# A decoder layer on one core: memory exponentials behind the value copies, rotation on VectorE, weight sums beside local attention, value transposes earlier

## The chip, the cores and the metric

One core of a Trainium2 chip runs the whole layer as one program. The metric is device microseconds of one execution; lower is better. The engines are TensorE (PE in the profile; PEld its weight loads), VectorE (DVE), ScalarE (ACT), GpSimd (POOL) and SyncE (SP), which only issues transfers. Each works through its own queue in order; what an instruction needs of another engine it waits for at the head of its queue.

## The reference, cut to what matters

The layer has a first feed-forward half step, a mixer of three branches (a recurrence, RWKV-7; sliding-window attention with rotary positions; cross-attention into 256 memory tokens), and a second feed-forward half step, for 1024 tokens of width 1024 in float32.

```
q_s = partial_rope(q_s, cos, sin); k_s = partial_rope(k_s, cos, sin)   # 16 of 64 dims of each head rotate
y_a = rwkv7_mix(p_rwkv, ...)                                           # state update token by token
y_b = sliding_window_gqa_sinks(q_s, k_s, v_s, sinks)                   # blocks of 128, the block and the one before
s = einsum('bshd,bmhd->bhsm', q * 128 ** -0.5, km); y_c = softmax(s) @ vm   # memory cross-attention
merged = g_a * (y_a @ w_branch[0]) + g_b * (y_b @ w_branch[1]) + g_c * (y_c @ w_branch[2])
h = h + rms_norm(merged @ w_out)
f2 = swiglu(rms_norm(h), ffn2_w_in, ffn2_w_out)
```

## The kernel before

**Products.** Large matrix products use a block form with 7 products where the plain one has 8, so sums of weight blocks and of activations are made first. Each factor is split into a high and a low part (`w_hi` by ACT at L304, `w_lo` by DVE at L306), and `mm3` (L381 to L383) gives three matmuls for each step of a product. The weight blocks arrive in five tiles `w_raw` by SP's queue; some eight operands (`OPS = 8`) are made ahead of PE. The accumulators lie in PSUM's eight banks, four for the large products (px, py, pz, po, pgate, pb, msc, mptr, mpv ...) and four for the rest (y, z, gram, bkt, sc, ptr, vtr, pv); a bank is taken again once its last reader is done.

**Order.** A scheduler lays down each engine's queue when the program is built. `high_priority(offset=...)` brings an instruction forward, `issue_after(x)` puts it behind x, `keep_in_program_order` fixes PE's order.

**The places of the change,** in the order of time:

- `win_pair` makes two strips of the mixer's input projection out of 7 products of 12 matmuls each (px, py, pz by turns). ACT copies px and pz into `part` (L1483), DVE adds `part` to the next accumulator into `att` (L1490), and ACT gives gates their tanh (L1493). Of its twelve pairs the seventh to the eleventh run beside `beside_pairs`, a generator from which the pairs draw one step (`between()`) behind each product. Its steps: three units of sums of the second feed-forward's output weights (for each, four loads of 256 KB, four adds on DVE at L675 to L678, four stores); the rotation's angle tables (`rope_tables`, two Sin activations on ACT, L1686 the second); and ten rotations of half a row, 128 x 512 each. A rotation (`rotate`, L1692 to L1694) is two multiplies and an add; those of row 0 (two) are made by DVE, the other eight by GpSimd. GpSimd's queue stores each (L720), and SP's loads the next half-row with its swapped copy into one of two pairs of buffers (`rope_x`, `rope_sw`).
- `rwkv_chain` goes through 16 chunks of 64 tokens. In a chunk PE makes z and y, the next chunk's value products (`values`, into the bank of y, which ACT copies to sv and uv at L1277), grams, and transposes (`turned`, bkt at L1297, which ACT copies to bk). Beside the chunks run eight `MemoryBlock`s of the cross-attention, one every two chunks: scores msc in chunk 2i + 1, maxima and four Exp activations (`powers`, L207) in the next (through the table `copied`, called once z is copied), the shares on DVE, then transposes and values.
- `attention` takes the eight blocks of the sliding window. Behind each block's scores (sc, L102) and transposes (ptr, L105) it puts some matmuls of the gate and branch products (`fill`, 46 steps a block, `LUMP = 46`). `turn_values` makes the transposes of v (vtr, L1961, two banks), two copies on ACT (vt, L1962) and a difference on DVE; it stands behind block 0's transposes.

Of the kernel before, what the change touches and what calls it, by code (L numbers as in the profile page):

```python
# [11 lines left out]
F32 = mybir.dt.float32  # L12
F32R = mybir.dt.float32r
I32 = mybir.dt.int32
ALU = mybir.AluOpType
# [3 lines left out]
P = 128  # L19
# [23 lines left out]
PAIR_UNITS = 3  # L43
# [137 lines left out]
class MemoryBlock(Block):  # L181
# [18 lines left out]

    def powers(self):
        V, S, st = self.nc.vector, self.nc.scalar, self.st
        scale = float(128 ** -0.5)
        V.tensor_scalar(st[:, 1], st[:, 0], -scale, None, ALU.mult)
        self.pr = self.pool.tile([P, 4, MEM], F32, tag="mp", name="mp", bufs=2)
        for i in range(4):
            S.activation(self.pr[:, i], self.banks[i // 2][:, (i % 2) * MEM : (i % 2 + 1) * MEM], ACT.Exp, scale=scale,  # L207
                         bias=st[:, 1, i : i + 1], accum_out=st[:, 2, i : i + 1])
# [27 lines left out]
class Builder:  # L236
# [364 lines left out]
    def ffn_in(self, f, x, form_d, first_d, parts, norm):  # L601

        nc, V = self.nc, self.nc.vector
        with self.tc.tile_pool(reuse_waits="tile", name="ffn_in", bufs=2) as pool:
# [13 lines left out]
            for j in range(KF):  # L618
                *pair, made = self.ffn_in_pair(f, j, pool, first_d)
                pairs.append(pair)  # L620
                skip = PAIR_UNITS if f == "ffn2" else 0
# [60 lines left out]
    def beside_pairs(self, pool, att_d):  # L682

        nc, V, G = self.nc, self.nc.vector, self.nc.gpsimd
# [3 lines left out]
        blocks = [t.rearrange("p (k c) -> p k c", c=P) for t in xs + sws]  # L688
# [22 lines left out]
        load(0)  # L711
        load(1)
        yield
        next(tables)
        yield
        for i, (row, h) in enumerate(rows):
            cols = slice(h * TH, (h + 1) * TH)
            self.rotate(V if row == 0 else G, xs[i % 2], sws[i % 2], cos[:, cols], sin[:, cols])
            yield
            nc.gpsimd.dma_start(att_d[row][:, cols], xs[i % 2])  # L720
            if i + 2 < len(rows):
                load(i + 2)
            if row:
                yield
# [522 lines left out]
    def rwkv_chain(self, pool, early, fetched, pk_d, inv_d, y, beside, copied, slot):  # L1247
# [23 lines left out]
        def values(n, ps):  # L1271

            for p, q in pairs:
                valued = mm(at(ps, p, 1 - q, W4), n["f"][ROWS[q], p, 4, :], self.center[ROWS[q]])
            for t in ("sv", "uv"):
                for q in (0, 1):
                    S.copy(n[t][ROWS[1 - q], q], v3(ps, W4)[ROWS[1 - q]])  # L1277
            return valued
# [40 lines left out]
        for c in range(NC_):  # L1319
# [25 lines left out]
            if not last:  # L1345
                values(nxt, py)
# [321 lines left out]
    def rope_tables(self, n, ang):  # L1668
# [6 lines left out]
        V.tensor_scalar(ang, ang, self.rope_c[:, 0:1], None, ALU.mult)  # L1675
        magic = 12582912.0
# [3 lines left out]
        for c in TWO_PI_PARTS:  # L1680
            V.scalar_tensor_tensor(ang, n, -c, ang, ALU.mult, ALU.add)
        V.tensor_scalar(ang, ang, 3.1415925, -3.1415925, ALU.min, ALU.max)
        V.scalar_tensor_tensor(n, ang, -1.0, ang, ALU.mult, ALU.max)
        yield
# [5 lines left out]
    def rotate(self, engine, x, sw, cos, sin):  # L1690

        engine.tensor_tensor(x, x, cos, ALU.mult)  # L1692
        engine.tensor_tensor(sw, sw, sin, ALU.mult)
        engine.tensor_tensor(x, x, sw, ALU.add)  # L1694
# [27 lines left out]
    def attention(self, blocks, turn_values):  # L1722

        self.fill(LUMP // 2, blocks[0].scores())
        blocks[0].soft(())
        for i, block in enumerate(blocks):
# [13 lines left out]
            if i == 0:  # L1740
                turn_values()
# [6 lines left out]
    def beside_chunks(self, i, block, copied, slot):  # L1748
# [7 lines left out]
        def scores():  # L1756
            block.scores()
            with self.tc.issue_after(self.kept.ins):
                for a in (0, 1) if late else (0,):
                    self.kept = block.most(a)  # L1760
                if late:
                    block.powers()
# [73 lines left out]
    def mixer(self, u, cp, close_raws, att_d, gate_d, km_d, vm_d):  # L1836
# [23 lines left out]
        with tc.tile_pool(reuse_waits="tile", name="gates", bufs=2) as gp:  # L1860
# [40 lines left out]
            with chunks, small("chain_y") as y_pool, small("memory") as mem_pool:  # L1901
                y = y_pool.tile([P, NPAIR, T], F32, name="y", bufs=1)
                blocks = [MemoryBlock(self, mem_pool, b, att_d=att_d, km=km, vm=vm, ahead=ahead, y_d=y_d[2]) for b in range(nb)]
                beside, copied, slot = {0: [lambda: nc.sync.dma_start(km, km_d), blocks[0].load, blocks[1].load, lambda: nc.sync.dma_start(vm, vm_d)]}, {}, {}
                for i, block in enumerate(blocks):
                    if i > 1:
                        beside[2 * i - 2] = [block.load]
                    self.beside_chunks(i, block, copied, slot)
# [8 lines left out]
                with small("chain") as pool:  # L1917
                    last = self.rwkv_chain(pool, early, fetched, pk_d, inv_d, y, beside, copied, slot)
# [26 lines left out]
            with stay, tc.tile_pool(reuse_waits="tile", name="att", bufs=1) as ap, tc.tile_pool(name="attw", bufs=2) as pool:  # L1945
# [7 lines left out]
                v_in = opened.enter_context(tc.tile_pool(reuse_waits="tile", name="v", bufs=1)).tile([P, T], F32, name="v_in")  # L1953
# [11 lines left out]
                self.attention(windows, turn_values)  # L1965
# [209 lines left out]
```

## Time and profile before

| | us |
|---|---|
| median of 3 runs | 2259.3 (2258.69 to 2261.74) |
| the profiled execution | 2259.9 |
| its span | 2258.2 |
| mean granted PE clock | 0.997 |
| ACT, busy | 1051.1 (47%) |
| POOL, busy | 118.7 (5%) |
| moved by DMA | 437.13 MB, 194 GB/s |

The profile covers one execution. A row of a timeline gives the start, the duration, the engine, the line of the kernel and the operation, and in brackets the idle time of that engine just before it with what ended it. Rows of ACTq or SPq are instructions of an engine's sequencer, mostly transfers that it issues. The pairs beside the rotation run from about 1040 to 1160 us, the chain from about 1185 to 1300, local attention from about 1315 to 1460.

### The profile page before, as it was taken

The page shows a single profiled execution, that of the slowest core. Times are in us where ns is not written, and L with a number is a line of the kernel's source. Part 1 is how long each engine was busy: PE and PEld are TensorE (multiplying, and loading weights), DVE is VectorE, ACT ScalarE, POOL GpSimd, SP SyncE. Part 2 cuts the span into 40 slices and gives each one's busy share as a digit, 9 for nine tenths or more (in the row PEclk, how much of TensorE's full clock was granted, in tenths as well). Part 3 has the DMA queues.
Part 4 walks back from the last instruction along what each step waited for, and adds up shares of the span by engine and source line. Part 5 has one row for each costly group of instructions (what it writes and reads, how often), then busy time and mean ns, then how long its engine had stood idle before and what let it go on. Part 6 is the DMA issues. An engine that isn't in the chain of part 4 may idle for free.

```text
span 2258.2 us, 34561 instructions
## 1 busy us (share of the span) xinstructions
PE 2217.0 (98%) x12244; PEld 1822.4 (81%) x12244; DVE 1680.1 (74%) x2790; ACT 1051.1 (47%) x1967; POOL 118.7 (5%) x187
## 2 busy tenths in 40 slices
PE   8999999999999999999999999999999999999998
PEld 6888888888887788888778877788888888888887
DVE  6988777766698887866747786794898887776676
ACT  6622333454556654444545574444663223345451
POOL 0000000000000011000432210000000000000000
PEclk9999999999999999999999999999999999999999
DMA  8565566686665456456664374464565555677763
GB/s 284 175 204 170 198 213 212 229 293 210 191 210 185 125 150 211 154 166 195 210 218 146 112 228 141 149 230 135 175 209 181 192 188 196 228 234 261 217 197 120
DMA packets 273628, 437.13 MB, mean 194 GB/s; under 512 B 51184, under 2 KB 89072, under 8 KB 273200
## 3 DMA queue, kind: packets, MB, share of 16 engines
q1 hardware_dynamic: 250752, 396.33, 54.4%
q10 hardware_dynamic: 20624, 34.94, 4.7%
q0 software_dynamic: 2080, 3.67, 0.5%
q8 instruction: 96, 1.57, 0.3%
q14 instruction: 76, 0.62, 0.1%
HBM read 295.90 MB, written 138.94 MB: 193 GB/s over the span
## 4 chain that ended last, share of the span: by engine, by line
PE 89%; DVE 5%; ACT 3%; DMA 2%; issue 1%; SPq 0%; ACTq 0%; DVEq 0%
PE px L381 9%; PE px L383 9%; PE px L382 9%; PE po L381 6%; PE po L383 6%; PE po L382 6%; PE pz L381 4%; PE pz L383 4%; PE pz L382 4%; PE pb L381 2%; PE pb L382 2%; PE pb L383 2%; PE pr L381 2%; PE pr L382 2%; PE pr L383 2%; PE pw L382 1%
## 5 line engine op out<-in xcount | busy, mean ns | idle before, releaser
L304 ACT CAST w_hi<-w_raw 128x512 fp32r<-128x512 f32 x618 | 382.3, 620 | 736.5 <-PE px L382 197.0
L306 DVE TENSOR_TENSOR w_lo<-w_raw,w_hi 128x512 fp32r<-128x512 f32 x618 | 428.6, 695 | 189.8 <-ACT w_hi L304 177.0
L381 PE MATMUL po<-u,w_hi 128*128 128x512 f32 (+1 forms) x476 | 180.9, 380 | 0.0
L382 PE MATMUL po<-u,w_hi 128*128 128x512 f32 (+1 forms) x476 | 180.9, 380 | 0.0
L383 PE MATMUL po<-u,w_lo 128*128 128x512 f32 (+1 forms) x476 | 180.9, 380 | 0.0
L381 PE MATMUL pz<-u,w_hi 128*128 128x512 f32 x400 | 156.0, 390 | 0.7 <-ACT part L1483 0.7
L381 PE MATMUL px<-u,w_hi 128*128 128x512 f32 x400 | 155.8, 390 | 0.8 <-DVE km L1658 0.8
L383 PE MATMUL px<-u,w_lo 128*128 128x512 f32 x400 | 155.8, 389 | 0.0
L383 PE MATMUL pz<-u,w_lo 128*128 128x512 f32 x400 | 155.7, 389 | 0.0
L382 PE MATMUL pz<-u,w_hi 128*128 128x512 f32 x400 | 155.6, 389 | 0.0
L382 PE MATMUL px<-u,w_hi 128*128 128x512 f32 x400 | 155.6, 389 | 0.0
L381 PE MATMUL px<-f,w_hi 128*128 128x512 f32 x352 | 137.2, 390 | 0.3 <-DVE up L783 0.3
L383 PE MATMUL px<-f,w_lo 128*128 128x512 f32 x352 | 137.0, 389 | 0.0
L382 PE MATMUL px<-f,w_hi 128*128 128x512 f32 x352 | 137.0, 389 | 0.0
L490 DVE TENSOR_TENSOR u<-hid,u 128x512 fp32r<-128x512 f32 x114 | 78.3, 689 | 47.2 <-ACT u L489 46.4
L382 PEld LDWEIGHTS po<-u,w_hi 128*128 128x128 f32 x476 | 89.5, 188 | 17.2
L383 PEld LDWEIGHTS po<-u,w_lo 128*128 128x128 f32 x476 | 89.5, 188 | 17.0
L381 PEld LDWEIGHTS po<-u,w_hi 128*128 128x128 f32 x476 | 89.5, 188 | 16.8
L489 ACT CAST u<-hid 128x512 fp32r<-128x512 f32 x114 | 70.7, 620 | 65.8 <-DMA hid<-form_d 57.7
L381 PEld LDWEIGHTS px<-u,w_hi 128*128 128x128 f32 x400 | 75.1, 188 | 17.0 <-ACT r L489 1.6
L381 PEld LDWEIGHTS pz<-u,w_hi 128*128 128x128 f32 x400 | 75.2, 188 | 16.7 <-ACT part L1483 1.1
L383 PEld LDWEIGHTS pz<-u,w_lo 128*128 128x128 f32 x400 | 75.1, 188 | 15.7
(461 smaller groups left out, 5265.0 us busy)
## 6 DMA issues: line engine op xcount, KB each, us to landing
w_raw<-in_ffn_in SPq DMA_DIRECT2D x224, 256.0 KB
hid<-form_d SPq DMA_DIRECT2D x154, 256.0 KB
w_raw<-in_win SPq DMA_DIRECT2D x112, 256.0 KB
form_d<-g SPq DMA_DIRECT2D x88, 256.0 KB
w_raw<-ffn_sum_d SPq DMA_DIRECT2D x88, 256.0 KB
ws<-in_ffn_out SPq DMA_DIRECT2D x76, 256.0 KB
ffn_sum_d<-ws SPq DMA_DIRECT2D x76, 256.0 KB
form_d<-h SPq DMA_DIRECT2D x66, 256.0 KB
```

Source lines behind the costliest of these rows:

```text
L304: self.nc.scalar.copy(hi, x)
L306: self.split_last = self.nc.vector.tensor_tensor(lo, x, hi.bitcast(F32), ALU.subtract)
L381: mm(out, wh, xh, start=first, stop=False, **kw)
L382: mm(out, wh, xl, start=False, stop=False, **kw)
L383: self.last_mm = mm(out, wl, xh, start=False, stop=last, **kw)
L489: self.nc.scalar.copy(hi, x)
L490: self.nc.vector.tensor_tensor(lo, x, hi.bitcast(F32), ALU.subtract)
```

## The change

1. In the chain, the four Exps of a memory block stand behind the next chunk's four value copies in ACT's queue instead of ahead of them; the small DVE operation ahead of them (`least`) stays where it was.
2. All ten rotations are made by VectorE. The tables come first, in six steps instead of four, with the two Sin activations next to each other; each rotation takes two steps. With the sums gone the whole takes 26 steps instead of 32.
3. The three units of weight sums leave `beside_pairs` and go to `attention`: loads in blocks 0, 2 and 4, adds and stores in blocks 1, 3 and 5, in four tiles `ws`. `PAIR_UNITS` is renamed `BLOCK_UNITS`.
4. `turn_values` stands behind block 0's scores and fill, ahead of block 1's scores.

```diff
@@ MemoryBlock
+    def least(self):
+        self.nc.vector.tensor_scalar(self.st[:, 1], self.st[:, 0], -float(128 ** -0.5), None, ALU.mult)
+
     def powers(self):
-        V, S, st = self.nc.vector, self.nc.scalar, self.st
+        S, st = self.nc.scalar, self.st
         scale = float(128 ** -0.5)
-        V.tensor_scalar(st[:, 1], st[:, 0], -scale, None, ALU.mult)
...
@@ beside_pairs
-        tables = self.rope_tables(cos, sin)
-        for q in range(PAIR_UNITS):
-            self.sums_loads("ffn2", q, blocks)
-            if q == 0:
-                next(tables)
-            yield
-            yield
-            self.sums_made("ffn2", q, blocks, self.split_last)
-            yield
-            if q < 2:
-                next(tables)
-            yield
         for t in sws:
-            G.memset(t, 0.0)
-        rows = [(0, h) for h in (0, 1)] + [(j, h) for j in range(2, 6) for h in (0, 1)]
+            nc.gpsimd.memset(t, 0.0)
+        rows = [(row, h) for row in (0, 2, 3, 4, 5) for h in (0, 1)]
...
-        load(0)
-        load(1)
-        yield
-        next(tables)
-        yield
+        for n, _ in enumerate(self.rope_tables(cos, sin)):
+            yield
+            if n in (4, 5):
+                load(n - 4)
         for i, (row, h) in enumerate(rows):
             cols = slice(h * TH, (h + 1) * TH)
-            self.rotate(V if row == 0 else G, xs[i % 2], sws[i % 2], cos[:, cols], sin[:, cols])
+            self.rotate(xs[i % 2], sws[i % 2], cos[:, cols], sin[:, cols])
             yield
             nc.gpsimd.dma_start(att_d[row][:, cols], xs[i % 2])
             if i + 2 < len(rows):
                 load(i + 2)
-            if row:
-                yield
+            yield
@@ rwkv_chain
-        def values(n, ps):
+        def values(n, ps, powers=()):
...
             for t in ("sv", "uv"):
                 for q in (0, 1):
-                    S.copy(n[t][ROWS[1 - q], q], v3(ps, W4)[ROWS[1 - q]])
+                    end = S.copy(n[t][ROWS[1 - q], q], v3(ps, W4)[ROWS[1 - q]])
+            with self.tc.issue_after(end.ins):
+                for f in powers:
+                    f()
...
-                values(nxt, py)
+                values(nxt, py, powers.get(c, ()))
@@ rope_tables
...
         V.scalar_tensor_tensor(n, ang, -1.0, ang, ALU.mult, ALU.max)
-        yield
         nc.scalar.activation(ang, ang, ACT.Sin)
         nc.scalar.activation(n, n, ACT.Sin, scale=-1.0, bias=self.half_pi)
...
-    def rotate(self, engine, x, sw, cos, sin):
-
-        engine.tensor_tensor(x, x, cos, ALU.mult)
-        engine.tensor_tensor(sw, sw, sin, ALU.mult)
-        engine.tensor_tensor(x, x, sw, ALU.add)
+    def rotate(self, x, sw, cos, sin):
+
+        V = self.nc.vector
+        V.tensor_tensor(x, x, cos, ALU.mult)
+        V.tensor_tensor(sw, sw, sin, ALU.mult)
+        V.tensor_tensor(x, x, sw, ALU.add)
@@ attention
-    def attention(self, blocks, turn_values):
+    def attention(self, blocks, turn_values, units):
 
         self.fill(LUMP // 2, blocks[0].scores())
+        turn_values()
         blocks[0].soft(())
...
                 blocks[i + 1].soft(block.copied)
-            if i == 0:
-                turn_values()
+            units[i % 2]()
             self.fill(LUMP - first, mm)
@@ beside_chunks
         if not late:
             add(copied, c + 1, lambda: block.most(1))
-            add(copied, c + 1, block.powers)
+            add(copied, c + 1, block.least)
+            add(powers, c + 1, block.powers)
@@ where attention is called
+                sums, loaded = iter(range(BLOCK_UNITS)), []
+
+                def load_unit():
+                    for q in itertools.islice(sums, 1):
+                        loaded.append((q, self.sums_loads("ffn2", q, self.sums_tiles(v_pool))))
+
+                def make_unit():
+                    while loaded:
+                        self.sums_made("ffn2", *loaded.pop(), self.split_last)
+
+                self.attention(windows, turn_values, (load_unit, make_unit))
```

In the order the rows have a line, an operation, what is written and read (numbers of buffers are given where they differ), and a shape. The changed kernel's lines are shifted: L1277 is L1264 there, L1297's copy to bk L1288, L207 L209, L1490 L1480, L1692 to L1694 L1686 to L1688, L306 L308, L331 to L337 L333 to L339, L1962 L1959, L1530 L1520, L489 L491.

ACT in the chain, from one chunk's output copy (y) on; before:

```order
L1308 COPY y<-y 128x4x64
L207 ACTIVATE mp,mst<-msc,mst 128x256 x4
L1277 COPY sv<-y 64x256 x2
L1277 COPY uv<-y 64x256 x2
L1298 COPY bk<-bkt 128x512
L1781 COPY yo<-mpv 128x512
L1782 DMA y_d<-yo 512x1x128
L1308 COPY y<-y 128x4x64
L1277 COPY sv<-y 64x256 x2
```

and now:

```order
L1298 COPY y<-y 128x4x64
L1264 COPY sv<-y 64x256 x2
L1264 COPY uv<-y 64x256 x2
L209 ACTIVATE mp,mst<-msc,mst 128x256 x4
L1288 COPY bk<-bkt 128x512
L1777 COPY yo<-mpv 128x512
L1778 DMA y_d<-yo 512x1x128
L1298 COPY y<-y 128x4x64
L1264 COPY sv<-y 64x256 x2
L1264 COPY uv<-y 64x256 x2
L1288 COPY bk<-bkt 128x512
```

The four Exps (mp) have gone from ahead of sv and uv to behind them, and ahead of bk.

DVE beside the fourth of these five pairs of products; before:

```order
L331 TENSOR_TENSOR part<-w_raw 128x512
L306 TENSOR_TENSOR w_lo<-w_raw,w_hi 128x512
L332 TENSOR_TENSOR w_raw<-w_raw 128x512
L1490 TENSOR_TENSOR att<-py,part 128x512
L333 TENSOR_TENSOR w_raw<-part,w_raw 128x512
L337 TENSOR_TENSOR w_raw<-w_raw 128x512
L306 TENSOR_TENSOR w_lo<-w_raw,w_hi 128x512
L306 TENSOR_TENSOR w_lo<-part,w_hi 128x512
L306 TENSOR_TENSOR w_lo<-w_raw,w_hi 128x512
L1490 TENSOR_TENSOR att<-px,part 128x512
```

and now:

```order
L1686 TENSOR_TENSOR rope_x_9898<-rope_x_9898,cos 128x512
L308 TENSOR_TENSOR w_lo<-w_raw,w_hi 128x512
L333 TENSOR_TENSOR part<-w_raw 128x512
L308 TENSOR_TENSOR w_lo<-w_raw,w_hi 128x512
L334 TENSOR_TENSOR w_raw<-w_raw 128x512
L1687 TENSOR_TENSOR rope_sw_9900<-rope_sw_9900,sin 128x512
L1480 TENSOR_TENSOR att<-py,part 128x512
L335 TENSOR_TENSOR w_raw<-part,w_raw 128x512
L1688 TENSOR_TENSOR rope_x_9898<-rope_x_9898,rope_sw_9900 128x512
L339 TENSOR_TENSOR w_raw<-w_raw 128x512
L308 TENSOR_TENSOR w_lo<-w_raw,w_hi 128x512
L308 TENSOR_TENSOR w_lo<-part,w_hi 128x512
```

Before, only weight operands (w_lo, part, w_raw) and the adds of att stood there, while GpSimd rotated; now the operations of the rotations stand between them, in the same queue.

ACT in local attention round the copies of vt; before:

```order
L163 COPY pt<-ptr 128x512
L489 CAST u<-yin 128x512
L148 ACTIVATE st<-st 128x8
L150 ACTIVATE sc,st<-sc,st 128x128 x5
L304 CAST w_hi<-w_raw 128x512
L150 ACTIVATE sc,st<-sc,st 128x128 x3
L1962 COPY vt<-vtr 128x512 x2
L1530 ACTIVATE gate<-pgate,half_gb 128x512
L131 COPY sc<-sc 128x256 x4
L304 CAST w_hi<-w_raw 128x512 x2
```

and now:

```order
L150 ACTIVATE sc,st<-sc,st 128x128
L148 ACTIVATE st<-st 128x8
L150 ACTIVATE sc,st<-sc,st 128x128 x7
L1520 ACTIVATE gate<-pgate,half_gb 128x512
L1810 DMA gin<-gate_d 128x512
L1959 COPY vt<-vtr 128x512 x2
L491 CAST u<-yin 128x512
L131 COPY sc<-sc 128x256
L1810 DMA gin<-gate_d 128x512
L131 COPY sc<-sc 128x256
```

The vt copies stood behind the eight Exps of block 1; now they stand behind those of block 0, ahead of the copies of block 1's scores (L131). On PE the eight vtr transposes, which stood directly behind block 0's ptr, stand directly ahead of block 1's sc.

More of the change, by code (lines that the diff above doesn't have):

```diff
@@ L42 @@
 KEEP = KP - OPS
-PAIR_UNITS = 3
+BLOCK_UNITS = 3
 RAWS = 5
@@ L682, in beside_pairs @@
     def beside_pairs(self, pool, att_d):
-        nc, V, G = self.nc, self.nc.vector, self.nc.gpsimd
+        nc = self.nc
         cos, sin = (pool.tile([P, T], F32, name=n, bufs=1) for n in ("cos", "sin"))
@@ L1903, in mixer @@
                 blocks = [MemoryBlock(self, mem_pool, b, att_d=att_d, km=km, vm=vm, ahead=ahead, y_d=y_d[2]) for b in range(nb)]
-                beside, copied, slot = {0: [lambda: nc.sync.dma_start(km, km_d), blocks[0].load, blocks[1].load, lambda: nc.sync.dma_start(vm, vm_d)]}, {}, {}
+                beside, copied, powers, slot = {0: [lambda: nc.sync.dma_start(km, km_d), blocks[0].load, blocks[1].load, lambda: nc.sync.dma_start(vm, vm_d)]}, {}, {}, {}
                 for i, block in enumerate(blocks):
@@ L1917, in mixer @@
                 with small("chain") as pool:
-                    last = self.rwkv_chain(pool, early, fetched, pk_d, inv_d, y, beside, copied, slot)
+                    last = self.rwkv_chain(pool, early, fetched, pk_d, inv_d, y, beside, copied, powers, slot)
                     self.held = []
@@ L1963, in turn_values @@
                     nc.vector.tensor_tensor(vd, vt[:, 1:], vt[:, : T // P - 1], ALU.subtract)
-                self.attention(windows, turn_values)
+                sums, loaded = iter(range(BLOCK_UNITS)), []
[6 more added lines that the diff above has]
+                self.attention(windows, turn_values, (load_unit, make_unit))
+                assert not loaded and next(sums, None) is None
                 for _ in self.fills:
```

19 lines of the change are left out of this document (12 added, 7 removed).

## The prediction

> **What bounds the kernel now.** I read the page first, for which engine is full; then PE's waits, for what the few idle microseconds wait for; then the timelines of PE and of the releasing engine round each of those waits.
>
> ```profile
> span 2258.2 us, 34561 instructions
> PE 2217.0 (98%) x12244; PEld 1822.4 (81%) x12244; DVE 1680.1 (74%) x2790; ACT 1051.1 (47%) x1967; POOL 118.7 (5%) x187
> ```
>
> TensorE (PE) is busy for all but 41.2 us of the span. The change takes no matmul away, so it can gain only idle time of PE and what a slower clock costs behind it. PE's waits, by releaser (total, times, longest):
>
> ```profile
> PE bkt L1297 <- ACT uv L1277: 7.5, 7, 1.1
> ...
> PE px L381 <- ACT part L1483: 6.1, 4, 2.5
> PE sc L102 <- ACT vt L1962: 2.2, 1, 2.2
> ...
> PE pz L381 <- ACT part L1483: 0.7, 1, 0.7
> ...
> PE z L1257 <- DVE sv L1355: 0.2, 1, 0.2
> ```
>
> What the change can reach is 7.5 in the chain, 6.1 + 0.7 beside the rotation, and 2.2 in local attention: 16.5 us. A wait can cost more than itself, which the clock shows (columns: window; busy time of PE, PEld, DVE, ACT, POOL; granted PE clock; DMA share; GB/s):
>
> ```profile
> 1120.00:1140.00 20.00, 17.30 (x68) 13.54 (x67) 15.14 (x12) 6.87 (x12) 16.93 (x15) 0.91 0.53 176
> 1330.62 0.39 PE L382 MATMUL pgate<-u,w_hi 128*128 128x512 f32 x1
> ...
> 1333.79 0.39 PE L381 MATMUL pgate<-u,w_hi 128*128 128x512 f32 x1
> ...
> 1131.05 0.39 PE L383 MATMUL pz<-mix_form,w_lo 128*128 128x512 f32 x1
> 1133.97 0.50 PE L381 MATMUL px<-mix_form,w_hi 128*128 128x512 f32 x1 [2.53 <-ACT part L1483]
> ...
> 1138.42 0.40 PE L381 MATMUL pz<-u,w_hi 128*128 128x512 f32 x1
> ```
>
> From 1330.62 to 1333.79 lie 14 matmuls in PE's steady stream, 0.2264 us each; a product of 12 takes 2.72. The 12 behind the wait of 2.53 took 1138.42 - 1133.97 = 4.45, so 1.73 more, at a granted clock of 0.91 for that window. Refilling PE costs a little too: 1131.05 to 1133.97 is 2.92, less the wait of 2.53 and a step of 0.23 leaves 0.16. The page "TensorE: Matmul & The Clock Gate" of the Trainium skill (the states table of its Part 1) has the clock drop after an idle window of about 3.4 us; by that a wait of 2.53 would leave the clock alone, and the sum below would be some 3 us smaller; here the rows decide.
>
> **Part 1: rotation by VectorE alone.** VectorE (DVE), GpSimd (POOL) and ScalarE (ACT) at the same moment:
>
> ```profile
> 1104.66 3.53 DVE L332 TENSOR_TENSOR w_raw<-w_raw 128x512 f32<-128x512 f32 x1
> 1108.11 0.68 DVE L1490 TENSOR_TENSOR att<-py,part 128x512 f32<-128x512 f32 x1
> 1109.92 3.49 DVE L337 TENSOR_TENSOR w_raw<-w_raw 128x512 f32<-128x512 f32 x1
> 1104.48 0.58 POOL L720 DMA_DIRECT2D att_d<-rope_x  x1 [0.30 <-POOL rope_x L1694]
> ...
> 1110.34 1.28 POOL L1692 TENSOR_TENSOR rope_x<-rope_x,cos 128x512 f32<-128x512 f32 x1
> 1108.82 0.72 ACT L1493 ACTIVATE att<-att,half_gb 128x512 f32<-128x512 f32 x1 [5.64 <-DVE att L1490]
> ```
>
> An addition of two SBUF tiles, 0.68 as a rule, takes 3.5 beside GpSimd's multiplies. The add of att (L1490) stands behind it in DVE's queue, the tanh behind that on ACT, and behind the tanh the copy of px that frees PE's bank; that is three of the four waits of px. The fourth is another chain on ACT: two Sin activations apart from each other, each with a table load in and out.
>
> ```profile
> 1080.40 1.28 ACT L1493 ACT_TABLE_LOAD   x1
> ...
> 1085.12 0.50 PE L381 MATMUL px<-mix_form,w_hi 128*128 128x512 f32 x1 [1.68 <-ACT part L1483]
> ```
>
> With both Sins adjacent two loads of 1.28 fall away: 2.56, more than the 1.68 that PE waited. They stand one pair of products earlier now, and could make px late there; the two activations and two loads are some 5 us against the 10.9 (4 products) in which that bank has to come free, so I cost them at nothing; the tables' vector operations are the same ones, cut into six steps. The pz wait of 0.7 follows weight loads that the queue of SP issued late behind the last rope store; rotations that end sooner remove it. Gain: 6.1 + 0.7 + 1.73 = 8.5, and 0.16 for refilling PE at each of the three other larger waits: 9.0.
>
> What is added: 8 rotations of 3 VectorE operations, 24 x 0.68 = 16.3 us of DVE in three pairs of 7 products (3 x 19.0 = 57 us), less the 12 adds of the moved sums (8.2). The window above had DVE busy for 15.14 of 20, but with 12 instructions; at 0.68 these are 8.2, so 8.1 net fit into what the slow operations leave. It costs nothing while that cover holds; if it fails, the att adds are late next.
>
> A cost not shown is DVE waiting for a half-row's transfer with the adds of att and the weight casts queued behind it. There are two buffers; each goes round by a store on GpSimd's queue and a load on SP's:
>
> ```profile
>   DMA rope_x<-att_d: 8.9, 4
> ```
>
> The buffer stored at 1104.48 is multiplied again at 1110.34 with no wait, so a round takes under 6; the four waits of 8.9 in total say that it is sometimes some 2 longer. Eight of the ten rotations now stand beside two pairs (38 us): 4.8 apart, 9.5 for a buffer, less 2 for its own three operations: 7.5, which holds the usual round and hardly the long one. Bounds: none of it reaches PE (0), or 8.9 does. I take 1.0, near the lower end: the usual round fits, and a bank of PE comes free with 1 to 2 us in hand by an estimate from the order and these durations.
>
> **Part 2: exponentials behind the value copies.** A chunk with them and one without, on ACT and on PE:
>
> ```profile
> 1207.16 0.48 ACT L207 ACTIVATE mp<-msc,mst 128x256 f32<-128x256 f32 x1
> ...
> 1207.75 0.74 ACT L1277 COPY sv<-y 64x256 f32<-64x256 f32 x2
> 1208.52 0.74 ACT L1277 COPY uv<-y 64x256 f32<-64x256 f32 x2
> 1207.55 0.69 PE L1257 MATMUL z<-uv,bk 128*64 128x64 f32 x16
> 1209.32 0.66 PE L1297 MATMUL bkt<-ident,f 128*128 128x128 f32 x4 [1.08 <-ACT uv L1277]
> 1215.63 0.69 PE L1257 MATMUL z<-uv,bk 128*64 128x64 f32 x16
> 1216.26 0.66 PE L1297 MATMUL bkt<-ident,f 128*128 128x128 f32 x4
> ```
>
> bkt takes the bank that the uv copies free. From z to bkt is 1.77 with the Exps ahead and 0.63 without: 1.14 each, seven times, 8.0. In the first chunk z at L1257 waits for DVE's sv (its row above) at nearly the same time and nothing is won; in the last, two weight casts now stand ahead of the copies, and I count half, 0.6. Gain 5 x 1.14 + 0.6 = 6.3. The Exps themselves come 1.5 us later (four copies of 0.37), and the bk copy behind them; bk is read in the next chunk, over 6 us on, so that covers it. Bounds: 0 and 8.0.
>
> **Part 3: value transposes earlier.**
>
> ```profile
> 1334.56 2.10 PE L102 MATMUL sc<-kd,qs 64*128 64x256 f32 x16
> 1336.59 0.50 PE L381 MATMUL pgate<-u,w_hi 128*128 128x512 f32 x1
> 1348.80 1.14 PE L102 MATMUL sc<-kd,qs 64*128 64x256 f32 x8
> 1352.12 1.83 PE L102 MATMUL sc<-kd,qs 64*128 64x256 f32 x8 [2.18 <-ACT vt L1962]
> 1353.88 0.79 PE L381 MATMUL pgate<-u,w_hi 128*128 128x512 f32 x1
> 1356.61 0.48 PE L381 MATMUL pgate<-u,w_hi 128*128 128x512 f32 x1
> ```
>
> Sixteen sc matmuls took 1353.88 - 1348.80 = 5.08 instead of 1336.59 - 1334.56 = 2.03, and the six behind them 2.73 instead of 6 x 0.2264 = 1.36: 4.4 us that go. Against it stands v_in:
>
> ```profile
> 1329.68 1.07 SPq L1954 DMA_DIRECT2D v_in<-att_d  x1
> 1330.84 2.64 SPq L1789 DMA_DIRECT2D yin<-y_d  x4
> 1337.69 0.62 ACT L489 CAST u<-yin 128x512 fp32r<-128x512 f32 x1 [0.25 <-DMA yin<-y_d]
> ```
>
> PE reaches the new place at 1334.5 of this clock, 4.8 us behind the load's issue. The second yin, issued at about 1331.5, was waited for until 1337.69, 6.2 on; v_in at that pace lands at 1335.8. New wait: 0 to 1.3; with the scores' last two banks now behind the vt copies, I take 1.0.
>
> **Part 4: weight sums in attention.** Twelve adds (4 x 0.60 a unit, start to start) come ahead of L166's multiplies in three blocks, where DVE idled for ACT. The shortest of the three stretches:
>
> ```profile
> 1410.28 1.29 DVE L166 TENSOR_TENSOR pt<-ptr,is_own 128x512 f32<-128x512 f32 x2 [2.58 <-ACT pt L163]
> ```
>
> The 2.4 of a unit fits. Their 24 transfers of 256 KB go into SP's queue ahead of weight loads, but eight operands of 2.72 us of PE each lie ahead of PE: 22 us of cover. Cost 0; if the cover fails, weight loads are late (third rival).
>
> **The sum**: 9.0 + 6.3 + 4.4 - 1.0 - 1.0 = 17.7 off the profiled execution's 2259.9, so 2242.2. That execution lies 0.6 above the median of the three runs shown, 2259.3, so the forecast is 17.1, or 0.76%, under it. Less than 0.2% (4.5 us) can't be told from no change here.
>
> **Rivals.**
> - DVE waits for the half-rows. For it: the 8.9 us above, and a margin gone where a round is long. Against: POOL's queue, no longer in arithmetic, issues each store at once. With three waits of 2 reaching PE and one slow-clock stretch of 1.7 in place of the 1.0, 6.7 more: 2248.9. The page "SBUF — State Buffer" of the Trainium skill (its box on DVE blocking DMA) has a transfer issued by GpSimd starve while VectorE holds the shared port, 620 ns becoming 3100; by these figures (an estimate) a store would take up to 2.5 us more, by this same route; no run here shows it yet.
> - The chain's wait only changes its name (ACT's late bk copy, or DVE's sv, as the 0.2 row hints). Against: chunks without Exps show no idle PE. The 6.3 go: 2248.5.
> - Slower: SP's queue blocks. Each unit of sums needs loads, adds and stores in turn through the same four tiles. If one unit holds up the weight loads for longer than the cover, PE starves; it decides once three units cost 17.7 / 3 = 5.9 each. At 6.5 plus 1.7 of slow clock each, 24.6: 2266.8. Against it: nothing on PE waits for w_raw in the rows above.
> - The GpSimd part does nothing, because ACT's own load makes px late; then only the Sin's 1.7 of the 9.0 come, and no new wait: 2259.9 - 1.7 - 6.3 - 3.4 = 2248.5. Against: DVE's 3.5 us rows.
>
> **Chances.** The forecast 0.62, the first rival 0.16, the second 0.07, the fourth 0.05, the third 0.05, and 0.05 for several small waits together that leave no change. Faster 0.62 + 0.16 + 0.07 + 0.05 = 0.90, of which I move 0.03 to no change, as margins of 1 to 2 us were worked out by hand: 0.87, 0.08, 0.05. Low end: no new waits (2.0) and the chain's full 8.0 instead of 6.3, 2238.5, and 1 for the run's spread: 2237.5. High end past the 2248.9 of the rivals, with two of them half true: 2253.
>
> **What would show it.** Right: no PE wait on part (L1483), uv or vt copies; DVE's additions at 0.68 throughout 1100 to 1140; granted clock 1.00 there; PE idle about 25 us. A wait of DVE for rope_x with PE idle behind it shows the first rival; PE idle on bkt or z in the chain the second; PE or ACT waiting for w_raw near the sums the third. The prediction is wrong if PE's idle time falls by less than 10 us.

## The result and the profile after

The changed kernel takes 2242.66 us, the median of 4 runs (2241.38 to 2243.76), against 2259.55 for the kernel before in the same comparison: 16.9 us less, a ratio of 0.9924 with a 95% interval of 0.9906 to 0.9941. The forecast was 2242.2. The profiled execution took 2241.38, of which 2239.7 are the span.

The top of the page after:

```profile
span 2239.7 us, 34573 instructions
PE 2211.1 (99%) x12244; PEld 1819.7 (81%) x12244; DVE 1677.6 (75%) x2814; ACT 1046.5 (47%) x1965; POOL 85.0 (4%) x163
```

PE's waits that are new or were at issue (total, times, longest):

```profile
PE z L1244 <- DVE sv L1345: 1.3, 1, 1.3
...
PE vtr L1958 <- DMA v_in<-att_d: 1.1, 1, 1.1
...
PE bkt L1287 <- ACT uv L1264: 0.3, 1, 0.3
PE px L383 <- ACT part L1473: 0.3, 1, 0.3
...
PE px L383 <- DVE att L1480: 0.2, 1, 0.2
```

PE's idle time fell by 12.6 us, from 41.2 to 28.6, where the prediction had about 25 left. The rest of the gain, 5.9, lies in PE's busy time, 2217.0 before and 2211.1 now, for the same 12244 matmuls. Some 4 of it are the two slow stretches that the prediction measured (1.73, and 4.4 less the wait of 2.18); where the other 2 lie stays open.

To see where the time went I cut the program at four matmuls that stand in both: the first px of the pairs beside the rotation, the first y of the chain, the first gup behind it, and the last ptr of local attention. Their starts, from PE's timeline, before and then after:

```profile
1039.63 0.39 PE L381 MATMUL px<-u,w_hi 128*128 128x512 f32 x1
1164.08 0.33 PE L1257 MATMUL y<-center,f 64*64 64x64 f32 x4
1303.46 0.48 PE L1414 MATMUL gup<-sg_hi,g_up 128*128 128x512 f32 x1
1449.39 0.30 PE L105 MATMUL ptr<-ident,sc 128*128 128x128 f32 x1 [0.41 <-DVE sc L154]
```

```profile
1039.50 0.39 PE L383 MATMUL px<-u,w_hi 128*128 128x512 f32 x1
1155.10 0.27 PE L1244 MATMUL y<-center,f 64*64 64x64 f32 x2
1288.10 0.47 PE L1404 MATMUL gup<-sg_hi,g_up 128*128 128x512 f32 x1
1430.71 0.30 PE L105 MATMUL ptr<-ident,sc 128*128 128x128 f32 x1 [0.42 <-DVE sc L154]
```

The differences of these starts give each stage's length:

| stage | before | after | won | forecast |
|---|---|---|---|---|
| pairs beside the rotation | 124.45 | 115.60 | 8.85 | 9.0 - 1.0 |
| chain | 139.38 | 133.00 | 6.38 | 6.3 |
| local attention | 145.93 | 142.61 | 3.32 | 4.4 - 1.0 |
| the sum of the three | 409.76 | 391.21 | 18.55 | 17.7 |

The three hold the whole gain of the profiled execution (2259.9 - 2241.38 = 18.5).

**Pairs.** The two windows that answer to the one shown of before (busy PE, PEld, DVE, ACT, POOL; clock; DMA; GB/s):

```profile
1100.00:1120.00 20.00, 19.69 (x87) 16.01 (x86) 17.23 (x28) 8.67 (x15) 2.16 (x4) 1.00 0.63 215
1120.00:1140.00 20.00, 20.00 (x90) 16.58 (x89) 10.70 (x17) 9.21 (x16) 0.55 (x1) 1.00 0.78 266
```

What DVE waited for in this stage:

```profile
DVE rope_x L1686 <- DMA rope_x<-att_d: 6.1, 5, 2.9
...
DVE rope_sw L1687 <- DMA rope_sw<-att_d: 2.4, 1, 2.4
```

Between 1120 and 1140 VectorE does 17 instructions in 10.70 us where it did 12 in 15.14: no operation on two 128x512 tiles takes longer than 0.69 in this stage. The granted clock is 1.00. DVE does wait 8.5 us for half-rows at the head of its queue, as the first rival had it, but all that PE waits here for the pairs' copies and adds (part and att) is 0.55 us (0.31 and 0.24).

**Chain.** ACT and PE in the second chunk with Exps, and PE's one new wait, in the first:

```profile
1198.42 0.74 ACT L1264 COPY uv<-y 64x256 f32<-64x256 f32 x2
1199.07 0.47 ACT L209 ACTIVATE mp<-msc,mst 128x256 f32<-128x256 f32 x1
...
1200.88 0.58 ACT L1288 COPY bk<-bkt 128x512 f32<-128x512 f32 x1
1198.57 0.69 PE L1244 MATMUL z<-uv,bk 128*64 128x64 f32 x16
1199.22 0.66 PE L1287 MATMUL bkt<-ident,f 128*128 128x128 f32 x4
...
1186.85 0.69 PE L1244 MATMUL z<-sv,gz 128*64 128x64 f32 x16 [1.26 <-DVE sv L1345]
```

From z to bkt is 0.65 (1.77 before), with the Exps behind uv. The first chunk with Exps, before:

```profile
1194.97 0.66 PE L1297 MATMUL bkt<-ident,f 128*128 128x128 f32 x4 [1.03 <-ACT uv L1277]
1195.83 0.69 PE L1257 MATMUL z<-sv,gz 128*64 128x64 f32 x16 [0.20 <-DVE sv L1355]
```

There the wait of 1.03 for uv became one of 1.26 for sv where 0.20 had been: nothing won.

**Attention.** The transposes in their new place:

```profile
1320.19 1.07 PE L1958 MATMUL vtr<-ident,v_in 128*128 128x128 f32 x8 [1.08 <-DMA v_in<-att_d]
1321.19 2.10 PE L102 MATMUL sc<-kd,qs 64*128 64x256 f32 x16
1323.22 0.50 PE L383 MATMUL pgate<-u,w_hi 128*128 128x512 f32 x1
```

PE waits 1.08 for v_in, and the sixteen sc behind it take 2.03, the full pace.

### The profile page after: what moved, and what is told of

Its sections match the earlier page's. It is cut to its first block, busy times and chain, and to the rows that moved or that the text cites. A ratio compares the mean times of both kernels' runs of the same rounds, so it can differ in the third digit from the quotient of the medians.

```text
span 2239.7 us, 34573 instructions
## 1 busy us (share of the span) xinstructions
PE 2211.1 (99%) x12244; PEld 1819.7 (81%) x12244; DVE 1677.6 (75%) x2814; ACT 1046.5 (47%) x1965; POOL 85.0 (4%) x163
## 4 chain that ended last, share of the span: by engine, by line
PE 92%; DVE 4%; DMA 2%; ACT 1%; issue 1%; SPq 0%; ACTq 0%; DVEq 0%
PE px L383 10%; PE px L385 10%; PE px L384 10%; PE po L383 6%; PE po L384 6%; PE po L385 6%; PE pz L383 4%; PE pz L385 4%; PE pz L384 4%; PE pb L383 2%; PE pb L384 2%; PE pb L385 2%; PE pr L383 2%; PE pr L384 2%; PE pr L385 2%; PE pw L385 1%
## 5 line engine op out<-in xcount | busy, mean ns | idle before, releaser
L306 ACT CAST w_hi<-w_raw 128x512 fp32r<-128x512 f32 x618 | 382.2, 620 | 728.2 <-PE px L384 198.2
L308 DVE TENSOR_TENSOR w_lo<-w_raw,w_hi 128x512 fp32r<-128x512 f32 x618 | 422.9, 686 | 183.9 <-ACT w_hi L306 168.7
L385 PEld LDWEIGHTS po<-u,w_lo 128*128 128x128 f32 x476 | 89.5, 188 | 17.1
L383 PEld LDWEIGHTS po<-u,w_hi 128*128 128x128 f32 x476 | 89.5, 188 | 16.9
L384 PEld LDWEIGHTS po<-u,w_hi 128*128 128x128 f32 x476 | 89.5, 188 | 16.9
L491 ACT CAST u<-hid 128x512 fp32r<-128x512 f32 x114 | 70.6, 620 | 66.2 <-DMA hid<-form_d 57.9
L383 PEld LDWEIGHTS px<-u,w_hi 128*128 128x128 f32 x400 | 75.1, 188 | 17.1 <-ACT r L491 1.6
```

The costliest lines, as they stand in the source:

```text
L306: self.nc.scalar.copy(hi, x)
L308: self.split_last = self.nc.vector.tensor_tensor(lo, x, hi.bitcast(F32), ALU.subtract)
L383: mm(out, wh, xh, start=first, stop=False, **kw)
L384: mm(out, wh, xl, start=False, stop=False, **kw)
L385: self.last_mm = mm(out, wl, xh, start=False, stop=last, **kw)
L491: self.nc.scalar.copy(hi, x)
```

## The experiments

Eleven kernels: each undoes one part of the change, does one part alone on the kernel before, or adds one thing; two of them add it to another of them. A stage's length is worked out as above, from each run's own trace. In the four traces that have the changed kernel's code in the stage of the pairs (the changed kernel, and the three runs that differ from it only in the chain or in attention) that stage took 115.60, 117.00, 117.07 and 116.25, and 115.24 with memsets added: between two single executions differences of under 2 us there tell nothing.

**Rotation back on GpSimd.**

```diff
-            self.rotate(xs[i % 2], sws[i % 2], cos[:, cols], sin[:, cols])
+            self.rotate(self.nc.vector if row == 0 else self.nc.gpsimd, xs[i % 2], sws[i % 2], cos[:, cols], sin[:, cols])
...
-    def rotate(self, x, sw, cos, sin):
-
-        V = self.nc.vector
+    def rotate(self, V, x, sw, cos, sin):
+
```

> The changed kernel, but the eight rotations of rows 2 to 5 go back to GpSimd; the Sins stay together, the sums stay in attention, the steps stay the same. Theory (GpSimd's operations slow VectorE's additions, and those make px late): additions of 3.5 us return beside the pairs, PE waits on part again for 3 to 6 us, with a stretch of slow clock where one wait is over 2; of the 8.8 us won up to the chain's start, 4 to 7 are lost: 2246.5 to 2250. The 1.68 us of the Sins stay won. Rival (the sums' leaving and the Sins did it): within 1 us of 2242.7, although additions are slow again.

Measured: 2246.61 us (2244.64 to 2247.58), ratio to before 0.9937 (0.9925 to 0.9949). The stage took 119.93, 2.9 to 4.7 more than in those five traces. DVE and PE there:

```profile
1090.30 3.52 DVE L308 TENSOR_TENSOR w_lo<-part,w_hi 128x512 fp32r<-128x512 f32 x1
...
1105.71 0.50 PE L383 MATMUL px<-mix_form,w_hi 128*128 128x512 f32 x1 [1.09 <-ACT part L1473]
...
1133.61 0.50 PE L383 MATMUL px<-mix_form,w_hi 128*128 128x512 f32 x1 [1.11 <-ACT part L1473]
```

The slow additions are back and px is late behind them, six times between 0.2 and 1.1. The rival (the sums' leaving and the Sins did it all) does not hold: all five executions lie above the changed kernel's four. The loss is at the lower edge of what was expected: none of these waits was over 1.11, and the granted clock stayed at 1.00.

**Work on GpSimd that nobody needs.** If the additions are slow because GpSimd works beside them, work whose result nobody waits for must do it too.

```diff
+        spare = pool.tile([P, TH], F32, name="spare", bufs=1)
+        nc.gpsimd.memset(spare, 0.0)
...
-            nc.gpsimd.dma_start(att_d[row][:, cols], xs[i % 2])
+            stored = nc.gpsimd.dma_start(att_d[row][:, cols], xs[i % 2])
+            with self.tc.issue_after(stored.ins):
+                for _ in range(3):                                     # pool_writes: range(8)
+                    nc.gpsimd.tensor_tensor(spare, spare, spare, ALU.mult)   # pool_writes: nc.gpsimd.memset(spare, 0.0)
```

> The changed kernel with 30 multiplies of a spare tile added on GpSimd's queue (three behind each half-row's store, 128 x 512, SBUF to SBUF; nothing reads them). The rotation stays on VectorE. Theory (an operation of GpSimd that reads SBUF holds up VectorE's additions of two SBUF tiles, whoever needs its result): additions of 1.7 to 3.5 us on VectorE again, GpSimd's multiplies longer than 1.3 where they meet, and 3 to 8 us lost up to the chain: 2246 to 2251. Rival (GpSimd's rotation hurt by handing over its result late, not by the operations beside it): additions stay at 0.69, under 1.5 lost.

> The same with 80 memsets of the spare tile, 0.53 us each, in place of the 30 multiplies: about as much of GpSimd's time, but nothing is read. Theory: VectorE's additions stay at 0.69; the stores stand behind up to 5 us of memsets, so VectorE waits somewhat longer for half-rows, and 0 to 2 us are lost: 2242.5 to 2244.7. Rival (any work on GpSimd slows VectorE): additions of over 1 us and 3 or more lost, as with the multiplies.

Measured: with multiplies 2255.2 (2252.51 to 2257.15), ratio 0.9982 (0.9971 to 0.9992); with memsets 2240.81 (2239.77 to 2244.37), ratio 0.992 (0.9902 to 0.9938). The stage took 127.88 and 115.24. With the multiplies, their own row (times in ns: least, median, most), then DVE's and PE's timeline, then a window:

```profile
L713 POOL TENSOR_TENSOR spare<-spare x30: 1039/1368/3008, 1076.3 to 1137.2; 128x512 f32<-128x512 f32 x30
```

```profile
1087.59 2.00 DVE L334 TENSOR_TENSOR w_raw<-w_raw 128x512 f32<-128x512 f32 x1
...
1116.59 0.79 PE L383 MATMUL px<-mix_form,w_hi 128*128 128x512 f32 x1 [3.29 <-ACT part L1478]
```

```profile
1100.00:1120.00 20.00, 16.71 (x67) 13.41 (x66) 17.04 (x22) 6.92 (x13) 13.64 (x12) 0.89 0.51 178
```

With the memsets, their row and the same window:

```profile
L713 POOL MEMSET spare<- x80: 524/527/548, 1073.9 to 1128.0; 128x512 f32 x80
```

```profile
1100.00:1120.00 20.00, 19.58 (x87) 15.90 (x86) 16.25 (x27) 8.64 (x15) 17.27 (x33) 1.00 0.53 178
```

With the multiplies 25 of VectorE's operations on two SBUF tiles take over 0.8 us (16 additions or subtractions and nine multiplies of the rotation), most of them some 1.5 and at most 2.00; the multiplies themselves are slowed up to 3.008. The rival, late results, is out. Memsets fill 17.27 of 20 us of GpSimd and slow nothing. And the eight additions of att between 1076 and 1138, which take one input from PSUM, keep 0.68 to 0.69 beside the multiplies (those that start at 1098.67 and 1137.57 lie wholly inside stretches of multiplies). So two SBUF inputs on VectorE's side and something that a multiply does and a memset does not are needed. The Trainium skill says what that is ("SBUF — State Buffer", "Who interferes with whom"): a VectorE instruction with two SBUF inputs contends with a GpSimd instruction that reads SBUF, not with one that only writes it. Both runs agree; a multiply differs from a memset in more than reading, and no run here parts the two. The size was missed: 12.3 us in the stage, not 3 to 8. PE waited three times for over 2 us, 7.7 in all (3.29, 2.30 and 2.15), and behind the first two stand slow matmuls, 12 and 8 of them.

**Only the rotation, on the kernel before.**

```diff
-            self.rotate(V if row == 0 else G, xs[i % 2], sws[i % 2], cos[:, cols], sin[:, cols])
+            self.rotate(V, xs[i % 2], sws[i % 2], cos[:, cols], sin[:, cols])
```

> The kernel before with one thing changed: all ten rotations on VectorE; sums, tables, steps and the rest as before. Theory: VectorE's additions take 0.7 throughout and the waits at 1111, 1126, 1134 and 1158 us mostly go; the wait at 1085 stays; 4 to 7 of the 8.85 us of this stage are won. Rival (without the moved sums VectorE is too full or waits for the half-rows): 0 to 3 won, with VectorE waiting for rope_x or rope_sw ahead of PE's waits.

Measured: 2251.43 (2250.52 to 2253.82), ratio 0.996 (0.9947 to 0.9974). The stage took 119.05: 5.4 of the 8.85. The whole is 8.3 faster than the kernel before; 2.25 of that lie in local attention (143.68 for 145.93), where nothing was changed. PE's waits there, and DVE's for half-rows:

```profile
1084.81 0.50 PE L381 MATMUL px<-mix_form,w_hi 128*128 128x512 f32 x1 [1.70 <-ACT part L1483]
...
1130.89 0.50 PE L381 MATMUL px<-mix_form,w_hi 128*128 128x512 f32 x1 [1.65 <-ACT part L1483]
```

```profile
DVE rope_x L1692 <- DMA rope_x<-att_d: 11.1, 6, 3.5
```

All additions are fast and the wait at 1085 stays, as expected; a new one at 1131 stands behind VectorE's waits: VectorE waited 3.46 for a half-row until 1125.43, and the add of att, the tanh and the copy of px came behind it, as in the first rival of the prediction.

**Only the Sins together, on the kernel before.**

```diff
-        V.scalar_tensor_tensor(n, ang, -1.0, ang, ALU.mult, ALU.max)
+        folded = V.scalar_tensor_tensor(n, ang, -1.0, ang, ALU.mult, ALU.max)
         yield
-        nc.scalar.activation(ang, ang, ACT.Sin)
-        nc.scalar.activation(n, n, ACT.Sin, scale=-1.0, bias=self.half_pi)
+        with self.tc.high_priority(offset=self.urgent), self.tc.issue_after(folded.ins):
+            nc.scalar.activation(ang, ang, ACT.Sin)
+            nc.scalar.activation(n, n, ACT.Sin, scale=-1.0, bias=self.half_pi)
```

> The kernel before with one thing changed: the two Sin activations stand next to each other on ACT, so two of the four table loads round them go. Theory: the wait of PE at 1085 us (1.68, with 0.16 to refill) goes and nothing else: 1.8 faster than before. Rival (the px copy is late there for other work on ACT): the wait shrinks by less than 0.5.

Measured: 2259.09 (2255.48 to 2266.73), ratio 1.0003 (0.999 to 1.0017). PE's waits in the stage:

```profile
1111.44 0.50 PE L381 MATMUL px<-mix_form,w_hi 128*128 128x512 f32 x1 [2.00 <-ACT part L1483]
1133.20 0.50 PE L381 MATMUL px<-mix_form,w_hi 128*128 128x512 f32 x1 [0.59 <-ACT part L1483]
1158.60 0.50 PE L381 MATMUL pz<-u,w_hi 128*128 128x512 f32 x1 [3.33 <-ACT part L1483]
```

The wait at 1085 is gone, so its cause is shown. But no gain is seen: the waits behind it, 1.76, 0.16, 2.53 and 0.72 before, are now 2.00, 0.59 and 3.33, and the stage took 125.22, no less than the 124.45 before. It looks as if PE came earlier to work that GpSimd and the transfers held at their own pace. This is one execution of a kernel whose executions lie between 2255 and 2267, and the interval of the ratio, 2.3 us faster to 3.8 slower, still holds the 1.8 that were expected; so that the wait bought nothing is not shown.

**The sums back beside the pairs**, in `rope_x` and `rope_sw` as before, with the tables' steps between them; then the same with the Sins put together as above.

```diff
+        blocks = [t.rearrange("p (k c) -> p k c", c=P) for t in xs + sws]
+        tables = self.rope_tables(cos, sin)
+        for q in range(BLOCK_UNITS):
+            self.sums_loads("ffn2", q, blocks)
+            next(tables)
+            yield
+            yield
+            self.sums_made("ffn2", q, blocks, self.split_last)
+            next(tables)
+            yield
+            yield
...
-        for n, _ in enumerate(self.rope_tables(cos, sin)):
-            yield
-            if n in (4, 5):
-                load(n - 4)
+        load(0)
+        load(1)
+        yield
...
+                load_unit = make_unit = lambda: None
                 self.attention(windows, turn_values, (load_unit, make_unit))
```

> The changed kernel, but the three units of weight sums stand beside the pairs again, ahead of the rotations, which then start some 7 products later; attention has none. Theory (room on VectorE is there; moving the sums was not what paid): PE's waits up to the chain's start grow by at most 2 us: 2242 to 2244.7. Rival (without their leaving VectorE and SP's queue would be too full: 12 additions and 24 transfers more in the stretch in which the rotations stand): waits of 1 to 2 us at three or more places, 2246 to 2250.

> The run with the sums beside the pairs again, now with the two Sin activations next to each other (there the queue had them apart, with four table loads, and PE waited 1.68 at that place). Theory: the sums themselves cost next to nothing there, and that wait was most of the 2 to 3.4 us lost: the wait of 1.68 goes, and the stage up to the chain takes 1.8 less than in that run; total 2242 to 2243.5. Rival (the additions and transfers cost it): the loss stays over 2 us, 2244.5 or more.

Measured: 2244.94 (2243.82 to 2250.84), ratio 0.9937 (0.9923 to 0.9952), and with the Sins together 2245.12 (2243.29 to 2246.12), ratio 0.9931 (0.9918 to 0.9944). The stage took 119.01 and 118.68; attention without sums 142.82 and 143.20, no less than the 142.61 with them. In the first run the queue of ACT had the Sins apart, and PE's waits on part and att were 1.68, 0.36 and 1.52; in the second the 1.68 is gone, and the waits are 0.47, 0.50, 0.90 and 1.13, 3.0 in all for 3.6. DVE's wait for half-rows in the second run:

```profile
DVE rope_x L1697 <- DMA rope_x<-att_d: 13.6, 6, 3.4
...
DVE rope_sw L1698 <- DMA rope_sw<-att_d: 2.4, 1, 2.4
```

16.0 us against 8.5: the theory fell in the second run. With the sums there the rotations start later and share the queue with 24 more transfers, and the stage takes 1.6 to 3.8 longer than in the five traces above. Which of the two does it was not tried apart. The medians are 2.3 and 2.5 over the changed kernel's, but the intervals of the ratios overlap with its own (0.9906 to 0.9941).

**The Exps ahead again.**

```diff
-            add(powers, c + 1, block.powers)
+            add(copied, c + 1, block.powers)
```

> The changed kernel, but the four Exps of a memory block stand ahead of the value copies again. Theory: bkt waits about 1.08 us for uv in six or seven chunks, of which the first costs nothing, since z waits for VectorE's sv at the same place; 6.3 us lost in the chain alone: 2249. Rival (part of the chain's 6.4 came from earlier stages, by weights or states that are ready earlier): 1 to 3 us lost, 2244 to 2246.

Measured: 2249.34 (2248.19 to 2252.62), ratio 0.9954 (0.994 to 0.9967). The chain took 139.74, 6.74 more, and the total is 6.7 over the changed kernel's. From PE's waits:

```profile
PE bkt L1287 <- ACT uv L1264: 7.8, 8, 1.1
```

and, of its timeline, the first chunk with Exps:

```profile
1187.34 0.66 PE L1287 MATMUL bkt<-ident,f 128*128 128x128 f32 x4 [1.04 <-ACT uv L1264]
1188.19 0.69 PE L1244 MATMUL z<-sv,gz 128*64 128x64 f32 x16 [0.19 <-DVE sv L1345]
```

In the first chunk 1.04 + 0.19 stands where the changed kernel waits 1.26: that wait only changes its name; the others are won, all but the 0.34 of the last.

**The transposes behind block 0's again.**

```diff
         self.fill(LUMP // 2, blocks[0].scores())
-        turn_values()
         blocks[0].soft(())
...
+            if i == 0:
+                turn_values()
             units[i % 2]()
```

> The changed kernel, but the value transposes stand behind block 0's transposes again. Theory: the wait of sc for vt of about 2.2 us is back with slow matmuls behind it (4.4 us in all), and the wait of 1.08 for v_in is gone: 3.3 us lost, 2246.0. Rival (the slow clock behind the wait came by chance in that one execution, and the wait alone counts): 2.2 - 1.1 = 1.1 lost, 2243.8.

Measured: 2247.35 (2246.86 to 2249.52), ratio 0.9944 (0.9932 to 0.9956): 4.7 over the changed kernel's median, and 5.46 in the stage (148.07). PE:

```profile
1337.99 2.55 PE L102 MATMUL sc<-kd,qs 64*128 64x256 f32 x8 [2.62 <-ACT vt L1960]
1340.47 0.79 PE L383 MATMUL pgate<-u,w_hi 128*128 128x512 f32 x1
...
1344.48 0.49 PE L383 MATMUL pgate<-u,w_hi 128*128 128x512 f32 x1
```

Eight sc take 2.48 instead of 1.02, and nine matmuls behind them 4.01 instead of 2.04: with the wait 6.05, less the 1.08 for v_in. The slow clock is no chance of one execution, but its price is not fixed: 1.46 + 1.97 = 3.4 us here, and 4.4 - 2.18 = 2.2 behind the same wait before.

**A place of its own for v_in**, then three buffers for the half-rows on top.

```diff
-                v_in = v_pool.tile([P, T], F32, name="v_in")
+                v_in = ahead.tile([P, T], F32, name="v_in", bufs=1)
```

```diff
-        half = lambda n: [pool.tile([P, TH], F32, name=f"{n}{i}", bufs=1) for i in (0, 1)]
+        half = lambda n: [pool.tile([P, TH], F32, name=f"{n}{i}", bufs=1) for i in range(3)]
...
-            if n in (4, 5):
-                load(n - 4)
+            if n > 2:
+                load(n - 3)
...
-            if i + 2 < len(rows):
-                load(i + 2)
+            if i + 3 < len(rows):
+                load(i + 3)
```

> The changed kernel with a place of its own for v_in, so that its load is issued ahead of the chain. Theory: PE's wait of 1.08 for v_in at the value transposes goes and no other takes its place: 1.2 faster than the changed kernel, 2241.4. Rival (the scores' banks behind the vt copies are late next): a wait of sc for vt of 0.3 to 1, gain under 0.7.

> The run with v_in's own place, and three buffers instead of two for the rotation's half-rows, loaded three ahead. Theory (what PE still waits there, 0.3 to 1.5 us, comes from VectorE waiting for half-rows): VectorE's waits for rope_x and rope_sw fall from some 8 us to under 2, no PE wait on part or att is left, and 0.5 to 2 us are won: 2239 to 2240. Rival (SP's queue is what is late, with more loads ahead of the weights now): PE waits shift to weights, no gain or 1 us lost: 2240.6 to 2242.

Measured: 2240.61 (2239.49 to 2243.46), ratio 0.9915 (0.9899 to 0.9932), and 2239.65 (2238.75 to 2242.19), ratio 0.9915 (0.9899 to 0.993). The first wins 1.12 in attention (141.49) and no wait takes the place of v_in's; by whole executions the intervals overlap with the changed kernel's. The second changes the pairs by nothing that can be told (116.09 against 116.25). DVE still waits, and PE once:

```profile
DVE rope_x L1686 <- DMA rope_x<-att_d: 5.6, 2, 4.0
```

```profile
1089.51 0.50 PE L383 MATMUL px<-mix_form,w_hi 128*128 128x512 f32 x1 [1.13 <-ACT part L1473]
```

6.2 us of waiting instead of 8.5, not the under 2 expected: neither theory holds as it stood, and what still delays the half-rows stays open.

## Why the prediction was right, and where not

- **The bound and the size.** Right: PE's idle time and its slow stretches were what there was to win. 17.7 were forecast off the profiled execution and 18.5 came; against the medians 17.1 and 16.9. To come so near took some luck: the kernel before ran between 2254.37 and 2267.84 in the other comparisons, and the sum was read from one execution.
- **Part 2, the Exps.** Right to 0.1 in sum and by its steps: the first chunk's wait renamed to VectorE's sv, five won whole, the last but for 0.34. Undoing it alone costs 6.7.
- **Part 3, the transposes.** Right: 3.4 forecast, 3.32 measured, and the new wait for v_in 1.08 where 1.0 was taken. That the size was so near has some luck in it: the slow stretch differs between executions (the stage took 143.68 in the run with only the rotation moved, where the vt wait was 1.68 and no clock fell, against 145.93 before).
- **Part 1, the rotation.** That GpSimd's multiplies slow VectorE's additions and make px late is shown by the multiplies and memsets and by the rotation put back. The total of the stage came out (8.0 forecast, 8.85 measured), but by the traces two terms in it were mis-sized and made up for each other. The step "with both Sins adjacent ... two loads fall away", 1.68 and its refilling: the wait does go, but alone it shows no gain (ratio 1.0003, with an interval that still holds the 1.8). And the sums' leaving was counted as VectorE's time only, at no gain to PE; with them back the stage is 1.6 to 3.8 longer. The rotation alone gives 5.4. Going on from there, the Sins put together give 0.4 (119.05 to 118.68, with the tables' steps moved too) and the sums' leaving 3.1 (118.68 to 115.60), each from single executions that scatter by nearly 2, so neither is shown by itself.
- **Part 4, the sums in attention.** Right: no cost there (142.61 with, 142.82 and 143.20 without), and PE's waits show none for weights.
- **The rivals.** The first was half there: VectorE waits 8.5 us for half-rows, nearly the 8.9 of GpSimd before, but its cover on PE's side held for all but 0.55. Of the 2.5 us more that its last sentence gave a store as an estimate, the median shows nothing: the ten stores issued by GpSimd landed after 3.3 us before (2.3 to 4.8) and 3.1 now (2.3 to 7.6); what held the longest one stays open. The figures of the Trainium skill that the estimate rests on ("SBUF — State Buffer", the box on DVE blocking DMA and the section behind it) are for a VectorE copy in a mode that takes two ports, which the rotation's multiplies and additions are not. The second came true in one chunk of seven, for which no gain had been counted. The third, SP's queue, did not show. The fourth, that the GpSimd part does nothing, is out: the rotation alone gives 5.4 in the stage, and putting it back costs 2.9 to 4.7.
- **The clock.** The prediction counted slow matmuls behind the waits of 2.53 and 2.18 (1.73 and 2.2 us), and such stretches are seen again behind like waits in other runs (below). The Trainium skill ("TensorE: Matmul & The Clock Gate", the states table of its Part 1) has the clock drop after an idle window of some 3.4 us; by that both terms would fall out of the sum, nearly 4 us and not the 3 that the prediction gave. The traces differ from it, and the rows decided rightly.

## What to carry to other kernels

Where PE is 98% busy, read the few waits that are left one by one, and for each name what is late next before counting it as won: the Sins' wait was real and was removed, and by itself no gain from it could be seen. Keep elementwise work with SBUF inputs off GpSimd while VectorE adds SBUF tiles for the critical path; the memsets tried here cost nothing. Put the copies that free a bank ahead of work that only has a deadline later.

## What the runs showed of the hardware

A short idle of PE already costs clock. In the thirteen traces (the two kernels and the eleven above), the wait at the program's start left out, 26 waits of PE last 1.3 us or more. None of the 13 from 1.3 to 1.76 us had slow matmuls within 10 us behind it; of the nine from 2.00 to 3.33 eight had 5 to 12 matmuls of some 0.43 us each, start to start, instead of 0.23, and one of 2.15 had none. The four in between (1.84 to 1.96) come at one place, near 781 us, ahead of the stages looked at above: three had slow matmuls behind them and one, of 1.85 in the changed kernel, had none. The 10 us round that place, first with the wait of 1.96 (rotation back on GpSimd), then with that of 1.85:

```profile
776.00:786.00 10.00, 8.04 (x29) 6.19 (x28) 9.35 (x13) 5.13 (x8) 2.26 (x5) 0.83 0.60 165
```

```profile
776.00:786.00 10.00, 8.15 (x36) 6.42 (x35) 9.46 (x13) 5.12 (x8) 2.25 (x5) 1.00 0.60 167
```

So the step lies near 2 us in these kernels and is no sharp one: slow matmuls are seen from a wait of 1.84 on, yet waits of 1.85 and 2.15 went without. What else decides is not shown. The three stretches worked out above cost 1.73, 2.2 and 3.4 us more than the wait itself.

GpSimd and VectorE slow each other: GpSimd's multiplies went from 1.04 to as much as 3.008 us beside VectorE's operations on two SBUF tiles, and additions of two such tiles on VectorE from 0.69 to as much as 3.53 beside GpSimd's rotations.
